# Attention outputs of blocks 1 to 3 in a tile of their own, and block 2's normed tokens transposed ahead through DRAM

## The chip, the core and the metric

The kernel runs on one core of a Trainium2 chip. The metric is the device time of one execution in microseconds (us); the kernel before takes 2342.25 us, the median of 3 runs that lie between 2341.23 and 2342.68.

## What is computed

One layer of a bidirectional encoder. 2,048 tokens and 16 meta tokens in front of them, 1,024 wide, in fp32:

```python
hn   = rms_norm(h, g_mix)
proj = hn @ w_in                      # q: 4 heads, k and v: 2 heads each, u: 4 Fourier groups
attn = block_attention(rope(rms_norm(q)), rope(rms_norm(k)), v)     # every token sees every token
four = fourier_mix(u, w_fourier)      # real part of a 2D DFT over tokens and channels
h    = h + concat(rms_norm(attn, g_attn_out), rms_norm(four, g_fourier_out)) @ w_out
h    = h + relu(rms_norm(h, g_mlp) @ w_up) ** 2 @ w_down            # d_ff = 4096
out  = rms_norm(h, g_final)[meta tokens dropped]
```

## The kernel before, in words

**Arithmetic.** Each fp32 operand of a matmul is split into a high and a low part: ACT makes the high part (a CAST, or an ACTIVATE with a scale, L68 and L71), DVE subtracts it from the source for the low part (L69, L72). A product is then three matmuls, high by high, high by low and low by high (`mm3`, L78 to L80). `split` is such a pair of ACT and DVE instructions. A raw weight tile `wr_...` is loaded through SP's queue and split into `wh_...` and `wl_...` (`wtile`); the rings hold 3 raw tiles (tag `wr`) and 4 of each part (tags `wh` and `wl`), 128x512 each.

**Stages.** Up to about 310 us: projections, norms and rope. Then the Fourier half, beside the first attention units. From there the 2,048 tokens are worked in four blocks of 512 (`BLOCKS`, numbered 0 to 3). Attention is 16 units, two heads of 256 queries each, four units to a block; a unit's result goes to the DRAM tensor `o_d[block]` as high and low parts, one slice of 128x512 for each head `k`. `mix(head(0), ...)` and `mix(head(1), ...)` run the MLP of blocks 0 and 1, and at each `yield` advance attention as far as a schedule says (`n0` and `n1` are the numbers of these yields). When a block's units are done, `out_a(b)` (L917 to L986) runs at the next chance: it loads the block's tokens `h`, multiplies the attention outputs by the attention half of `w_out` in two halves of 512 columns (4 heads by 4 token tiles, PSUM tiles `poa`), adds to `h`, and takes the norm's factor: ACT squares (`hj`), DVE adds up, GpSimd raises to the power -1/2 (`rs_m`, L983). Blocks 2 and 3 then store `h` to `h_d` (L985).

**The operands of `out_a`.** For block 0 they are one tile `at_0` of 16 KB per partition, in the place `e0` of the pool `ey`, which is free then; each slice is loaded once and serves both halves. For blocks 1 to 3, `attn` (L939 to L945) loads each slice into `ath_...` and `atl_...`, tiles of the rings `wh` and `wl`, which they share with the weights, and loads it again for the second half: 8 slices by 2 halves by 3 blocks, 48 loads of 256 KB.

**The transposed tokens.** The MLP needs the normed tokens with the model dimension on the partitions. For blocks 0 and 1, `transposes` (L988) scales them on ACT (`m`, L997), transposes on PE (`pmt`, L1002) and splits the result into `mT` in `e0` (high) and `e1` (low) of `ey`, which thus hold block 1's operands until `up(1, 7)` ends. For blocks 2 and 3 the MLP is one Strassen-Winograd product over both blocks, 7 products for 8: its token operands are the raw transposed tiles `b11`, `b21` (block 2) and `b12`, `b22` (block 3), and the seven forms made of them (`bf1` to `bf7`; `b_form`, a split of 128x1024 pieces); its weight operands are made by `up_weights` (`wuh`, `wul`) from tiles `R0` and `R1`. `flip` (L1162) makes the raw tiles: DVE scales the tokens in place (L1166), PE transposes (L1170), ACT scales out of PSUM (L1171).

**The order at the hand-over.** After both `mix` calls come `down(1, 6)` and `out_a(3)`; then block 2's tokens are loaded again from `h_d` into `h2_0` and `h2_1`, in the places of `R0` and `R1` (L1175 to L1180); then `up(1, 7)` runs with the two flips between its steps, `up_weights` makes its first four weight forms, forms `1` (in `e0`) and `2` (in `e1`) are split, and `down(1, 7)` runs its two halves with form `5` between and form `6` behind. The tokens' activations of `up` are relu, square and a split (L1028, L1029, L68, L69). `b22t`, a sum used for form `6`, has its own tile in the pool `rb`.

**What sets the order.** The program is written once, and a scheduler orders each engine's instructions by cost and priority; within an engine they then run in that order. A tile's buffer is handed on when its last reader is done. Loads run through SP's queue in order, so that one that waits for its buffer holds up those behind it; attention's loads run through GpSimd's queue. The score tiles `s` and the transposes `pmt` share a PSUM ring of two (tag `S` of `app`).

Of the kernel before, what the change touches and what calls it, by code (L numbers as in the profile page):

```python
# [133 lines left out]
def encoder_block(ctx: ExitStack, tc: tile.TileContext, x, meta, w_in, w_f,  # L134
# [63 lines left out]
    h_d = [dram.tile([P, D], F32, name=f"h_d{t}") for t in range(NT)]  # L198

# [709 lines left out]
    hps = hp0, Lines(tc.alloc_tile_pool(name="hp1", bufs=1, reuse_waits="tile"), small)  # L909
    mp = Lines(tc.alloc_tile_pool(name="mp", bufs=1, reuse_waits="tile"), small)  # L910
# [5 lines left out]
    def out_a(b):  # L916
# [16 lines left out]
        if b == 0:  # L933
            A = ey.tile([P, 2, NQ, 512], R32, name="at_0", tag="e0")
            for k in range(NQ):
                for e in range(2):
                    nc.sync.dma_start(f32v(A[:, e, k]), o_d[b][:, e, k])

        def attn(half, k):  # L939
            if b == 0:  # L940
                return A[:, 0, k], A[:, 1, k]
            a = [wp.tile([P, 512], R32, name=f"at{e}_{b}_{half}_{k}", tag="w" + e, bufs=4) for e in "hl"]
            for e in range(2):
                nc.sync.dma_start(f32v(a[e]), o_d[b][:, e, k])
            return a  # L945

        part = []
        for half in range(2):
# [9 lines left out]
            for k in range(NQ):  # L958
                w = wtile(w_out[k * P:(k + 1) * P, c], f"oa_{b}_{half}_{k}", c_ao(k))
                ops[k] = attn(half, k), w  # L960
# [27 lines left out]
    def transposes(b):  # L988
# [5 lines left out]
        for kk in range(KT // 2):  # L994
# [3 lines left out]
            for i in range(2):  # L998
# [4 lines left out]
                split(mhl[0][:, k, :T * P], mhl[1][:, k, :T * P], ps[:, :T * P], c_mlp(k))  # L1003
            yield
# [75 lines left out]
    def head(b):  # L1080
# [14 lines left out]
        def ahead():  # L1095
            if todo and att.n >= need[todo[0]] + 2:
                yield from out_a(todo.pop())
# [9 lines left out]
    n0, n1 = 8 + 4 + 8 * 15 + 8, 8 + 8 * 13 + 8  # L1107
# [67 lines left out]
    h2 = []  # L1175
    for i in range(2):
        h = sp.tile([P, 2, D], F32, name=f"h2_{i}", tag=f"R{i}")
        for t in range(2):
            nc.sync.dma_start(h[:, t], h_d[8 + 2 * i + t])
            h2.append(h[:, t])  # L1180
    b11, b21 = (ra.tile([P, 4, 512], F32, name=f"b{i}1", tag=f"b{i}1") for i in (1, 2))
    b12, b22, b22t = (rb.tile([P, 4, 512], F32, name=f"b{i}2", tag=f"b{i}2") for i in (1, 2, 3))
    BF = {}

# [24 lines left out]

    def in_pool(pool, name):  # L1210
        t = pool.tile([P, 8, 512], R32, name="bf" + name, tag="bf" + name)
        return [t[:, 0:2], t[:, 2:4]], [t[:, 4:6], t[:, 6:8]]

    def flips():
        yield from flip(2, h2, (b11, b21))
        yield from flip(3, H.pop(3), (b12, b22))

    fl = flips()
# [5 lines left out]
    b_form("1", in_ey(0), b11)  # L1224
# [114 lines left out]
    sl.release()  # L1339
    for p in hps[::-1]:  # L1340
# [267 lines left out]
```

## Time and profile before

| | |
|---|---|
| median of 3 runs (lowest, highest) | 2342.25 us (2341.23, 2342.68) |
| the profiled execution, its time | 2340.36 us |
| its span, first to last instruction | 2338.5 us |
| mean granted clock of TensorE | 0.996 |
| PE busy | 2298.0 us, 98% |
| DVE, ACT, GpSimd busy | 74%, 55%, 7% |
| moved by DMA | 312.56 MB, 134 GB/s |

Busy times are of one execution, each engine on its own; a share near 100% says that the engine rarely stood still, not that its matmuls came at the best pace. The rows by windows show how many instructions started in a stretch of time (in brackets, with an x), the clock granted to TensorE in it (PEclk) and the DMA engines' share. The rows of waits give engine, instruction and line, what it waited for, the microseconds in total, how often, and the longest.

### The profile page before, as it was taken

What the parts mean: (1) busy time and instruction counts of PE and PEld (TensorE: products, weight loads), DVE (VectorE), ACT (ScalarE), POOL (GpSimd) and SP (SyncE); (2) the same over time, 40 slices, a digit from 0 to 9 for tenths busy, and PEclk for the clock granted to TensorE, in tenths of its full rate; (3) what the DMA queues carried; (4) which work ended last, traced back from release to release, by engine and by line L of the source; (5) the groups of instructions that cost most, each with busy time, mean ns of one, the idle gap of its engine ahead of it and who ended that gap; (6) DMA issues with size and microseconds to landing.
All of it is one profiled execution on the core that took longest, in us unless ns stands there. A gap on an engine that the chain in (4) does not pass through costs nothing.

```text
span 2338.5 us, 30433 instructions
## 1 busy us (share of the span) xinstructions
PE 2298.0 (98%) x10774; PEld 1875.1 (80%) x10774; DVE 1720.1 (74%) x2771; ACT 1276.6 (55%) x2395; POOL 165.7 (7%) x211
## 2 busy tenths in 40 slices
PE   8999999999999999999999999999999999999998
PEld 7889887677788888788878788888788888788886
DVE  5435678988777887877897877885685656596786
ACT  6443356644565665566776566663655555443333
POOL 2212120110100000100010100000000000100000
PEclk9999999999999999999999999999999999999999
DMA  6333252543533222443242553224535444764442
GB/s 207 104 112 108 73 156 76 170 148 129 169 115 109 78 86 86 142 130 109 64 167 86 169 180 108 64 83 151 185 117 185 153 144 165 303 209 158 130 133 81
DMA packets 181225, 312.56 MB, mean 134 GB/s; under 512 B 15328, under 2 KB 64192, under 8 KB 180944
## 3 DMA queue, kind: packets, MB, share of 16 engines
q1 hardware_dynamic: 162736, 269.97, 35.2%
q0 software_dynamic: 18336, 40.64, 5.9%
q8 instruction: 85, 1.39, 0.2%
q14 instruction: 68, 0.56, 0.1%
HBM read 232.66 MB, written 77.89 MB: 133 GB/s over the span
## 4 chain that ended last, share of the span: by engine, by line
PE 80%; DMA 2%; DVE 2%; ACT 2%; issue 1%; POOL 0%; SPq 0%; POOLq 0%; DVEq 0%; ACTq 0%
PE pdn L78 5%; PE pdn L80 5%; PE pdn L79 5%; PE pup L80 5%; PE pup L79 5%; PE pup L78 5%; PE o L770 3%; PE ux L78 2%; PE ux L80 2%; PE s L78 2%; PE ux L79 2%; PE s L79 2%; PE s L80 2%; PE dx L78 2%; PE dx L79 2%; PE dx L80 2%
## 5 line engine op out<-in xcount | busy, mean ns | idle before, releaser
L78 PE MATMUL pdn<-wh_dn,ah 128*128 128x512 f32 x512 | 201.3, 396 | 2.1 <-ACT r L1028 1.2
L78 PE MATMUL pup<-mT,wh_up 128*128 128x512 f32 x512 | 201.7, 394 | 0.0
L80 PE MATMUL pup<-mT,wl_up 128*128 128x512 f32 x512 | 200.5, 392 | 0.0
L79 PE MATMUL pdn<-wl_dn,ah 128*128 128x512 f32 x512 | 200.5, 392 | 0.0
L79 PE MATMUL pup<-mT,wh_up 128*128 128x512 f32 x512 | 200.4, 391 | 0.0
L80 PE MATMUL pdn<-wh_dn,al 128*128 128x512 f32 x512 | 200.3, 392 | 0.0
L755 ACT ACTIVATE S<-S 128x512 f32<-128x512 f32 (+1 forms) x261 | 162.6, 629 | 59.3 <-DVE S L749 57.8
L749 DVE TENSOR_TENSOR S<-S,mb 128x512 f32<-128x512 f32 (+1 forms) x272 | 180.9, 683 | 16.4 <-ACT mb L742 16.3
L713 ACT COPY S<-s 128x512 f32<-128x512 f32 (+1 forms) x272 | 158.2, 583 | 57.0 <-PE s L80 51.0
L720 DVE TENSOR_TENSOR M<-M,S 128x512 f32<-128x512 f32 (+1 forms) x240 | 165.0, 687 | 26.8 <-ACT S L713 24.0
L68 ACT CAST wh_up<-wr_up 128x512 fp32r<-128x512 f32 x128 | 79.0, 620 | 141.5 <-PE pup L79 75.9
L69 DVE TENSOR_TENSOR wl_up<-wr_up,wh_up 128x512 fp32r<-128x512 f32 x128 | 87.3, 686 | 68.0 <-ACT wh_up L68 60.4
L68 ACT CAST wh_dn<-wr_dn 128x512 fp32r<-128x512 f32 x128 | 79.3, 620 | 101.4 <-PE pdn L80 52.9
L69 DVE TENSOR_TENSOR wl_dn<-wr_dn,wh_dn 128x512 fp32r<-128x512 f32 x128 | 87.6, 686 | 60.8 <-ACT wh_dn L68 52.1
L78 PE MATMUL s<-q,kt 128*128 128x512 f32 (+1 forms) x272 | 128.1, 471 | 3.5 <-ACT S L755 2.1
L68 ACT CAST ah<-a 128x1024 fp32r<-128x1024 f32 x56 | 58.4, 1048 | 112.7 <-issue 60.8
L69 DVE TENSOR_TENSOR pl<-S,ph 128x512 fp32r<-128x512 f32 x165 | 112.5, 686 | 9.7 <-ACT ph L68 7.7
L78 PEld LDWEIGHTS pdn<-wh_dn,ah 128*128 128x128 f32 x512 | 96.7, 189 | 25.3 <-ACT r L1028 4.6
L68 ACT CAST ph<-S 128x512 fp32r<-128x512 f32 x165 | 101.3, 617 | 27.7 <-PE o L80 23.1
L776 DVE TENSOR_TENSOR acc<-acc,S 128x512 f32<-128x512 f32 x165 | 112.8, 683 | 0.4 <-ACT S L755 0.4
L80 PEld LDWEIGHTS pdn<-wh_dn,al 128*128 128x128 f32 x512 | 96.3, 188 | 20.1 <-DVE al L69 0.4
L79 PEld LDWEIGHTS pdn<-wl_dn,ah 128*128 128x128 f32 x512 | 96.5, 188 | 19.5
(322 smaller groups left out, 6339.0 us busy)
## 6 DMA issues: line engine op xcount, KB each, us to landing
wr_up<-in_w_up_dram SPq DMA_DIRECT2D x128, 256.0 KB, 2.8
wr_dn<-in_w_down_dram SPq DMA_DIRECT2D x128, 256.0 KB, 2.6
a<-s_d SPq DMA_DIRECT2D x42, 512.0 KB, 3.7
R<-in_w_up_dram SPq DMA_DIRECT2D x16, 1024.0 KB, 5.3
s_d<-s SPq DMA_DIRECT2D x64, 256.0 KB, 2.0
d<-in_w_down_dram SPq DMA_DIRECT2D x26, 512.0 KB, 5.0
s_d<-c SPq DMA_DIRECT2D x48, 256.0 KB, 2.3
h<-h_d SPq DMA_DIRECT2D x20, 512.0 KB, 5.3
```

Of the source, the lines that this page charges most:

```text
L68: nc.scalar.copy(hi, src)
L69: nc.vector.tensor_tensor(lo, src, f32v(hi), op=ALU.subtract)
L78: nc.tensor.matmul(out, a[0], b[0], start=first, stop=False, skip_group_check=chain)
L79: nc.tensor.matmul(out, a[0], b[1], start=False, stop=False, skip_group_check=chain)
L80: nc.tensor.matmul(out, a[1], b[0], start=False, stop=last, skip_group_check=chain)
L713: nc.scalar.copy(S[:rows], ps[:rows])
L720: nc.vector.tensor_tensor(M[:rows], M[:rows], S[:rows], op=ALU.max)
L749: nc.vector.tensor_tensor(S, S, s["mb"][:rows], op=ALU.subtract)
L755: nc.scalar.activation(p, S, AF.Exp, scale=ISQ)
L770: nc.tensor.matmul(s["O"], v[:, i % 4], p, start=i == 0, stop=False)
L776: nc.vector.tensor_tensor(acc, acc, p, op=ALU.add)
```

## The change

- A pool `atp` with one tile of 16 KB (tag `at`) holds the attention outputs of blocks 1, 2 and 3 in turn, in the form that block 0 had: 8 loads of 256 KB a block, each slice once, both halves of `out_a` read it. `attn` goes, and the rings `wh` and `wl` hold weights alone.
- `flip_early(2)` follows `out_a(2)` inside `head(1)`: for each pair of slices of the model dimension, four ACT scalings of 128x256, eight transposes into the PSUM ring of the scores, two ACT scalings out of PSUM and two stores of 256 KB to the DRAM tensor `m_d`, and a yield (four in all, so `n1` is 124 for 120). `flip(2)` goes: 4 scalings of 128x1024 on DVE, 32 transposes and 8 scalings out of PSUM between the steps of `up(1, 7)`; `flip(3)` stays there. `b11` and `b21` are loaded from `m_d`, 1 MB each; the reload of block 2's tokens (4 loads of 512 KB) goes, so `R0` and `R1` are free for the weights earlier.
- Form `1` is made in the tile `at`, which is free after `out_a(3)`, instead of in `e0`, which is free only after `up(1, 7)`; `b22t` moves into `e0`. The pool `rb` shrinks by 8 KB, and `atp` is released at the end of the seven products.

```diff
@@ -196,6 +196,7 @@
     v_n = dram.tile([P, NKV, NT, P], F32, name="v_n")
     v_m = dram.tile([MR, NKV, P], F32, name="v_m")
     h_d = [dram.tile([P, D], F32, name=f"h_d{t}") for t in range(NT)]
+    m_d = dram.tile([P, KT, 512], F32, name="m_d")
 
 
     def tbank(name, shape=(P, 512)):
@@ -907,6 +908,7 @@
 
 
     hps = hp0, Lines(tc.alloc_tile_pool(name="hp1", bufs=1, reuse_waits="tile"), small)
+    atp = Lines(tc.alloc_tile_pool(name="atp", bufs=1, reuse_waits="tile"), small)
     mp = Lines(tc.alloc_tile_pool(name="mp", bufs=1, reuse_waits="tile"), small)
     H, MT = {}, {}
 
@@ -930,19 +932,10 @@
         nc.vector.tensor_copy(ss[:, :T], ps)
         ra = rstd_of(mp, ss[:, :T], T, 512, "a")
         sums = [mp.tile([P, 2], F32, name=f"hss_{b}_{t}", tag="hss", bufs=8) for t in range(T)]
-        if b == 0:
-            A = ey.tile([P, 2, NQ, 512], R32, name="at_0", tag="e0")
-            for k in range(NQ):
-                for e in range(2):
-                    nc.sync.dma_start(f32v(A[:, e, k]), o_d[b][:, e, k])
-
-        def attn(half, k):
-            if b == 0:
-                return A[:, 0, k], A[:, 1, k]
-            a = [wp.tile([P, 512], R32, name=f"at{e}_{b}_{half}_{k}", tag="w" + e, bufs=4) for e in "hl"]
+        A = (atp if b else ey).tile([P, 2, NQ, 512], R32, name=f"at_{b}", tag="at" if b else "e0")
+        for k in range(NQ):
             for e in range(2):
-                nc.sync.dma_start(f32v(a[e]), o_d[b][:, e, k])
-            return a
+                nc.sync.dma_start(f32v(A[:, e, k]), o_d[b][:, e, k])
 
         part = []
         for half in range(2):
@@ -957,7 +950,7 @@
 
             for k in range(NQ):
                 w = wtile(w_out[k * P:(k + 1) * P, c], f"oa_{b}_{half}_{k}", c_ao(k))
-                ops[k] = attn(half, k), w
+                ops[k] = (A[:, 0, k], A[:, 1, k]), w
                 if k < NQ - 2:
                     for t in range(T):
                         products(t, k)
@@ -1001,6 +994,23 @@
                 for t in range(T):
                     nc.tensor.transpose(ps[:, t * P:(t + 1) * P], m[t // 2][:, t % 2, i * P:(i + 1) * P], ident)
                 split(mhl[0][:, k, :T * P], mhl[1][:, k, :T * P], ps[:, :T * P], c_mlp(k))
+            yield
+
+    def flip_early(b):
+
+        hs, ms = H.pop(b), MT[b]
+        for kk in range(KT // 2):
+            m = [a_tile(f"m_{b}_{i}_{kk}").rearrange("p (t e) -> p t e", t=2) for i in range(2)]
+            for t in range(4):
+                nc.scalar.activation(m[t // 2][:, t % 2], hs[t][:, kk * 256:(kk + 1) * 256], AF.Copy, scale=ms[t])
+            for i in range(2):
+                k = 2 * kk + i
+                ps = app.tile([P, 512], F32, name=f"pmt_{b}_{k}", tag="S", bufs=2)
+                for t in range(4):
+                    nc.tensor.transpose(ps[:, t * P:(t + 1) * P], m[t // 2][:, t % 2, i * P:(i + 1) * P], ident)
+                raw = a_tile(f"mt_{b}_{k}")
+                nc.scalar.activation(raw, ps, AF.Copy, scale=c_mlp(k))
+                nc.sync.dma_start(m_d[:, k], raw)
             yield
 
     def up(b, grp):
@@ -1094,7 +1104,10 @@
 
         def ahead():
             if todo and att.n >= need[todo[0]] + 2:
-                yield from out_a(todo.pop())
+                c = todo.pop()
+                yield from out_a(c)
+                if c == 2:
+                    yield from flip_early(c)
 
         for grp in range(8 if b == 0 else 7):
             yield from up(b, grp)
@@ -1104,7 +1117,7 @@
                 yield from ahead()
         assert not todo
 
-    n0, n1 = 8 + 4 + 8 * 15 + 8, 8 + 8 * 13 + 8
+    n0, n1 = 8 + 4 + 8 * 15 + 8, 8 + 8 * 13 + 8 + 4
     a0, a2 = need[0] + LEAD, need[3] + 1
     a1 = a0 + (a2 - a0) * n0 // (n0 + n1)
     att.cap = need[0] + AHEAD
@@ -1172,15 +1185,12 @@
             if k % 2:
                 yield
 
-    h2 = []
-    for i in range(2):
-        h = sp.tile([P, 2, D], F32, name=f"h2_{i}", tag=f"R{i}")
-        for t in range(2):
-            nc.sync.dma_start(h[:, t], h_d[8 + 2 * i + t])
-            h2.append(h[:, t])
     b11, b21 = (ra.tile([P, 4, 512], F32, name=f"b{i}1", tag=f"b{i}1") for i in (1, 2))
-    b12, b22, b22t = (rb.tile([P, 4, 512], F32, name=f"b{i}2", tag=f"b{i}2") for i in (1, 2, 3))
+    b12, b22 = (rb.tile([P, 4, 512], F32, name=f"b{i}2", tag=f"b{i}2") for i in (1, 2))
+    b22t = ey.tile([P, 4, 512], F32, name="b32", tag="e0")
     BF = {}
+    for b, k in ((b11, 0), (b21, 4)):
+        nc.sync.dma_start(b, m_d[:, k:k + 4])
 
     def b_form(name, tiles, src):
 
@@ -1207,21 +1217,21 @@
         return tuple([wp.tile([P, 1, 512], R32, name=f"bf{e}{name}_{i}", tag="w" + e, bufs=4) for i in range(4)]
                      for e in "hl")
 
+    def in_at(name):
+        t = atp.tile([P, 2, 4, 512], R32, name="bf" + name, tag="at").rearrange("p l k n -> p (l k) n")
+        return [t[:, 0:2], t[:, 2:4]], [t[:, 4:6], t[:, 6:8]]
+
     def in_pool(pool, name):
         t = pool.tile([P, 8, 512], R32, name="bf" + name, tag="bf" + name)
         return [t[:, 0:2], t[:, 2:4]], [t[:, 4:6], t[:, 6:8]]
 
-    def flips():
-        yield from flip(2, h2, (b11, b21))
-        yield from flip(3, H.pop(3), (b12, b22))
-
-    fl = flips()
+    fl = flip(3, H.pop(3), (b12, b22))
     for _ in up(1, 7):
         next(fl, None)
     drain(fl)
     UW = up_weights()
     ready = [next(UW) for _ in range(4)]
-    b_form("1", in_ey(0), b11)
+    b_form("1", in_at("1"), b11)
     b_form("2", in_ey(1), b21)
     drain(down(1, 7, (0,)))
     minus(b11, b12, b11)
@@ -1337,6 +1347,7 @@
     pc.release()
     sl4.release()
     sl.release()
+    atp.release()
     for p in hps[::-1]:
         p.release()
     wp.release()
```

Three places show how instructions move. First SP's queue where block 1's attention outputs are loaded (`o_d` is the DRAM tensor, `wr_oa` the raw weights of `w_out`'s attention half), before and then after:

```order
L793 DMA o_d1_3464<-oh_7_9125 128x2x256
L793 DMA o_d1_3464<-ol_7_9126 128x2x256
L881 DMA wr_oa_1_0_0_9457<-in_w_out_dram 128x512
L881 DMA wr_oa_1_0_1_9496<-in_w_out_dram 128x512
L881 DMA wr_oa_1_0_2_9535<-in_w_out_dram 128x512
L944 DMA ath_1_0_0_9463<-o_d1_3464 128x512
L944 DMA atl_1_0_0_9464<-o_d1_3464 128x512
L881 DMA wr_oa_1_0_3_9545<-in_w_out_dram 128x512
L881 DMA wr_oa_1_1_0_9637<-in_w_out_dram 128x512
L944 DMA atl_1_0_1_9503<-o_d1_3464 128x512
L944 DMA ath_1_0_1_9502<-o_d1_3464 128x512
L944 DMA ath_1_0_2_9541<-o_d1_3464 128x512
```

```order
L882 DMA wr_oa_1_0_0_9453<-in_w_out_dram 128x512
L794 DMA o_d1_3465<-oh_7_9197 128x2x256
L794 DMA o_d1_3465<-ol_7_9198 128x2x256
L938 DMA at_1_9440<-o_d1_3465 128x512 x4
L882 DMA wr_oa_1_0_1_9488<-in_w_out_dram 128x512
L882 DMA wr_oa_1_0_2_9506<-in_w_out_dram 128x512
L882 DMA wr_oa_1_0_3_9512<-in_w_out_dram 128x512
L882 DMA wr_oa_1_1_0_9600<-in_w_out_dram 128x512
L882 DMA wr_oa_1_1_1_9635<-in_w_out_dram 128x512
L882 DMA wr_oa_1_1_2_9670<-in_w_out_dram 128x512
```

The loads of `ath` and `atl`, spread between the weights, are now one load `at_1` of four slices, directly behind the store of the last unit (four more stand further ahead in the queue), and the weights follow in one run.

Second, ACT's order at the hand-over from `up(1, 7)` to `down(1, 7)` (`r` and `ah` are the activations of its four feature tiles, `pup` and `pmt` PSUM tiles, `wuh` weight forms, `b22` block 3's raw tile), before and then after:

```order
L1028 ACTIVATE r_1_7_0_16404<-pup_1_7_0_16152 128x512
L1029 ACTIVATE r_1_7_0_16404<-r_1_7_0_16404 128x512
L68 CAST ah_1_7_0_16407<-r_1_7_0_16404 128x512
L1171 ACTIVATE b22_16150<-pmt_3_4_16368,cols_94 128x512
L1171 ACTIVATE b22_16150<-pmt_3_5_16374,cols_94 128x512
L1028 ACTIVATE r_1_7_1_16411<-pup_1_7_1_16153 128x512
L68 CAST wuh6_0_16448<-us2_0_16445 128x1024
L1029 ACTIVATE r_1_7_1_16411<-r_1_7_1_16411 128x512
L68 CAST wuh5_0_16452<-us1_0_16444 128x1024
L1171 ACTIVATE b22_16150<-pmt_3_6_16392,cols_94 128x512
L1171 ACTIVATE b22_16150<-pmt_3_7_16398,cols_94 128x512
L68 CAST ah_1_7_1_16414<-r_1_7_1_16411 128x512
```

```order
L1038 ACTIVATE r_1_7_0_16371<-pup_1_7_0_16171 128x512
L1039 ACTIVATE r_1_7_0_16371<-r_1_7_0_16371 128x512
L68 CAST ah_1_7_0_16374<-r_1_7_0_16371 128x512
L1038 ACTIVATE r_1_7_1_16378<-pup_1_7_1_16172 128x512
L1039 ACTIVATE r_1_7_1_16378<-r_1_7_1_16378 128x512
L68 CAST ah_1_7_1_16381<-r_1_7_1_16378 128x512
L68 CAST wh_dn_1_7_0_2_16479<-wr_dn_1_7_0_2_16477 128x512
L1038 ACTIVATE r_1_7_2_16385<-pup_1_7_2_16173 128x512
L68 CAST bf1_16428<-b21_16165 128x1024
L1039 ACTIVATE r_1_7_2_16385<-r_1_7_2_16385 128x512
L68 CAST bf1_16428<-b21_16165 128x1024
L68 CAST ah_1_7_2_16388<-r_1_7_2_16385 128x512
```

Before, four scalings out of PSUM and two weight forms of 128x1024 stand between the cast of tile 0 (`ah_1_7_0`) and that of tile 1 (`ah_1_7_1`); now the activations of tiles 0 and 1 stand in one run, and one weight cast and the two pieces of form `2` (`bf1`) are all that stands among those of tile 2. The scalings and the weight forms have moved ahead of these rows.

Third, PE's order at the first transposes of `flip_early(2)` (`o` and `s` are attention's products, `pup_1_2` is `up(1, 2)`); all of it is new here, since before no transposes stood in this stretch:

```order
L78 MATMUL pup_1_2_0_13278<-mT0_1_11385,wh_up_1_2_0_13284 128x512
L79 MATMUL o_12_12632<-pl_12_13_13203,vt_4_1_3_10126 128x512
L80 MATMUL o_12_12632<-ph_12_13_13202,vt_4_1_3_10126 128x512
L79 MATMUL pup_1_2_0_13278<-mT1_1_11386,wh_up_1_2_0_13284 128x512
L1010 MATMUL pmt_2_0_13145<-ident_96,m_2_0_0_13139 128x128
L1010 MATMUL pmt_2_1_13153<-ident_96,m_2_0_0_13139 128x128
L80 MATMUL pup_1_2_0_13278<-mT0_1_11385,wl_up_1_2_0_13285 128x512
L1010 MATMUL pmt_2_0_13145<-ident_96,m_2_0_0_13139 128x128
L1010 MATMUL pmt_2_1_13153<-ident_96,m_2_0_0_13139 128x128
L78 MATMUL pup_1_2_1_13279<-mT0_1_11385,wh_up_1_2_0_13284 128x512
L1010 MATMUL pmt_2_0_13145<-ident_96,m_2_1_0_13140 128x128
L1010 MATMUL pmt_2_1_13153<-ident_96,m_2_1_0_13140 128x128
```

The transposes stand 14 matmuls behind the last product of `out_a(2)`, each pair between two matmuls of `up(1, 2)`. On ACT the four scalings, the pair of scalings out of PSUM and the next four scalings follow one another with one or two of attention's instructions between, and the cast of weight `wh_up_1_2_3` stands behind the last scaling; PE first needs that weight 18 instructions after the last transpose.

## The prediction

> **What bounds the kernel now.** I read the page first.
>
> ```profile
> span 2338.5 us, 30433 instructions
> PE 2298.0 (98%) x10774; PEld 1875.1 (80%) x10774; DVE 1720.1 (74%) x2771; ACT 1276.6 (55%) x2395; POOL 165.7 (7%) x211
> PE 80%; DMA 2%; DVE 2%; ACT 2%; issue 1%; POOL 0%; SPq 0%; POOLq 0%; DVEq 0%; ACTq 0%
> ```
>
> PE sets the time: it is busy for 98% of the span, and 80% of the chain that ended last is on it. The change takes no matmul away and adds none, since the 32 transposes of block 2 only move. So all that it can win is time in which PE stands still or runs at a lower clock, and 2338.5 - 2298.0 = 40.5 us of idle time is the ceiling for the first. The waits of PE show whose it is.
>
> ```profile
> PE pt L253 <- ACT x L237: 8.9, 2, 8.2
> PE poa L78 <- DMA ath<-o_d: 6.7, 10, 1.8
> PE dy L79 <- DVE bl L69: 2.1, 1, 2.1
> PE s L78 <- ACT S L755: 2.1, 1, 2.1
> PE dx L78 <- ACT ah L68: 1.9, 1, 1.9
> PE pdn L78 <- ACT r L1028: 1.2, 1, 1.2
> PE pdn L78 <- ACT ah L68: 0.8, 1, 0.8
> PE uy L78 <- ACT bf L68: 0.6, 1, 0.6
> ```
>
> The first row is the start of the kernel. Two rows belong to the change: `poa` waits ten times for the loads of `ath`, 6.7 us, and `pdn` and `uy`, at the hand-over from `up(1, 7)` to `down(1, 7)`, wait 1.2 + 0.8 + 0.6 = 2.6 us for ACT. `dx` and `dy` lie near 2030 and 2045 us, in the joint down product, which the change does not reach. Next the table of windows, with an undisturbed stretch first, then the three `out_a`, the hand-over, and the two short stretches at a lower clock.
>
> ```profile
> 700.00:728.00 28.00, 28.00 (x125) 23.20 (x124) 24.80 (x41) 15.41 (x27) 1.44 (x2) 1.00 0.38 114
> 960.00:988.00 28.00, 25.17 (x102) 19.67 (x101) 21.37 (x37) 14.22 (x29) 0.76 (x1) 0.94 0.58 177
> 1308.00:1336.00 28.00, 25.30 (x108) 19.77 (x107) 23.20 (x40) 16.41 (x32) 1.45 (x2) 1.00 0.60 186
> 1636.00:1660.00 24.00, 22.68 (x98) 17.32 (x98) 13.40 (x27) 11.82 (x27) 2.95 (x4) 1.00 0.78 261
> 1676.00:1704.00 28.00, 25.40 (x114) 19.89 (x113) 26.64 (x29) 24.56 (x41) 0.00 (x0) 0.94 0.16 57
> 976.00:980.00 4.00, 4.00 (x12) 3.15 (x11) 1.37 (x3) 1.65 (x3) 0.00 (x0) 0.57 0.33 114
> 1692.00:1696.00 4.00, 3.81 (x10) 3.01 (x11) 4.00 (x6) 3.67 (x7) 0.00 (x0) 0.61 0.13 43
> ```
>
> The undisturbed stretch starts a matmul each 28.00 / 125 = 0.224 us. The count shows the loss better than the busy column, because a matmul's modelled duration (389 to 396 ns in other rows of the page) is longer than this pace, so an idle time looks shorter than what is lost. It also catches the two stretches with PEclk 0.57 and 0.61, where PE counts as busy at half pace.
>
> **What the change can win.** By counts, `out_a(1)` lacks 23 matmuls, 5.2 us (960 to 988); `out_a(2)` lacks 17, 3.8 us (1308 to 1336); `out_a(3)` has 98 where 24.00 / 0.224 = 107 would start, 9 x 0.224 = 2.0 us (1636 to 1660). At the hand-over 24 of the 114 records are transposes, which start much closer together:
>
> ```profile
> 1676.00:1704.00 28.00, 3.05 (x24) 2.60 (x23) 0.00 (x0) 3.81 (x6) 0.94 0.16 57
> 1683.20 1.03 PE L1170 MATMUL pmt<-ident,h 128*128 128x128 f32 x8
> 1683.99 0.48 PE L78 MATMUL pdn<-wh_dn,ah 128*128 128x512 f32 x1
> 1685.22 0.39 PE L80 MATMUL pdn<-wh_dn,al 128*128 128x512 f32 x1
> 1686.38 0.50 PE L78 MATMUL pdn<-wh_dn,ah 128*128 128x512 f32 x1 [0.77 <-ACT ah L68]
> 1690.22 0.73 PE L78 MATMUL uy<-bf,wuh 128*128 128x512 f32 x2 [0.61 <-ACT bf L68]
> 1692.18 0.50 PE L78 MATMUL pdn<-wh_dn,ah 128*128 128x512 f32 x1 [1.23 <-ACT r L1028]
> ```
>
> Eight transposes take 1683.99 - 1683.20 = 0.79 us, 0.1 us each. So 90 x 0.224 + 24 x 0.1 = 22.6 of the 28.0 us are used and 5.4 are lost. The sum by counts is 5.2 + 3.8 + 2.0 + 5.4 = 16.4 us. A lower bound comes from the busy columns: 2.83 + 2.70 + 1.32 + 2.60 = 9.4 us idle, and the two slow stretches lack 17.9 - 12 and 17.9 - 10 starts, 1.3 and 1.8 us, the second partly idle: about 12 us. Some records can be missing, which makes the counts too generous; I take 14.5 us as what is there to win, between 12 and 16.4 and nearer to the counts.
>
> *The waits of `out_a`.* These rows say why `ath` comes late: the load itself is short, and its buffer is what is awaited.
>
> ```profile
> ACT wh_oa L71 <- PE poa L79: 9.4, 4, 3.6
> ath<-o_d SPq DMA_DIRECT2D x24, 256.0 KB, 3.1
> atl<-o_d SPq DMA_DIRECT2D x24, 256.0 KB, 3.5
> o_d<-oh SPq DMA_DIRECT2D x16, 256.0 KB, 2.3
> ```
>
> The first row is ACT's wait from 1300 to 1340: the weights' high parts, in the same ring of four as `ath`, stand still until `poa` gives a tile back. Four tiles hold two steps' worth of weight and operand, so a load can only be issued when the product two steps back is done, and lands 3.1 us later, against 12 matmuls, 2.7 us, of a step. With a tile of its own the whole operand is asked for at once, and the rings hold four steps of weights. What stays is the distance from the last unit's store, 2.3 us, and the load, 3.5 us, to the first product: in the new order 88 and 116 PE rows stand between that unit's last transposition and the products with heads 0 and 2 in `out_a(1)`, some 20 us at 0.224 each; `out_a(2)` has 98 rows for its late heads, `out_a(3)` 103. `out_a(0)`, which works in this form already, has no row at all among PE's waits. I leave 0.7 us of the 11 (bounds 0 and 3), mostly for the weights, which now have the ring alone.
>
> *The hand-over.* PE waits there for ACT, which is 24.56 of 28.00 us busy, with DVE at 26.64. From these engines the change takes block 2's share:
>
> ```profile
> L1171 ACT ACTIVATE b<-pmt,cols x16: 672/682/705, 1658.6 to 1685.1; 128x512 f32<-128x512 f32 x16
> L1166 DVE TENSOR_SCALAR h<-h,rs_m 128x1024 f32<-128x1024 f32 x3 | 2.3, 752 | 1.3 <-DMA h_d<-h 1.3
> L68 ACT CAST bf<-b 128x1024 fp32r<-128x1024 f32 x6 | 6.4, 1064 | 0.0
> ```
>
> ACT loses 8 x 0.682 = 5.5 us, DVE 4 x 0.752 = 3.0. Besides, the four weight forms are made before `out_a(3)`, and block 3's scalings end some 24 matmuls ahead of the end of `up(1, 7)`. So after `pup` of tile 0 is done, 18 matmuls or 4.1 us remain on PE; ACT needs about 3 x 0.5 for tile 0, 3 x 0.5 for tile 1, a weight cast, and for tile 2 the same and two casts of 1.06: some 7.1 us from the end of tile 0, and PE asks for tile 2 at 4.1 + 24 x 0.224 = 9.5 us. The cover is 2 us. I leave 0.8 us of the 5.4 (bounds 0 and 4). What is late next is form `6`, behind `down(1, 7)` as before.
>
> The half pace goes with the waits if the waits cause it: both slow stretches follow directly on an idle time of PE of 1 to 2 us. The Trainium skill (TensorE: Matmul & The Clock Gate, in the section Why this matters for your kernels) sees it otherwise: it warns of idle gaps of over about 3 us, and no gap here is that long. By that rule the slow stretches would have another cause and stay, and the sum would be about 3 us less; that is a rival below.
>
> **What the change adds.** *`flip_early(2)`* puts on ACT 16 scalings of 128x256 and 8 out of PSUM, in a stretch with attention. Their like stands behind `out_a(0)`:
>
> ```profile
> L997 ACT ACTIVATE m<-h,rs_m x32: 493/502/518, 637.5 to 1173.3; 128x256 f32<-128x256 f32 x32
> 637.46 2.90 ACT L997 ACTIVATE m<-h,rs_m 128x256 f32<-128x256 f32 x7
> 640.26 1.24 ACT L71 ACTIVATE mT<-pmt,cols 128x512 fp32r<-128x512 f32 x2
> 636.00:648.00 12.00, 12.00 (x57) 7.96 (x56) 6.53 (x12) 11.71 (x28) 2.90 (x4) 1.00 0.46 134
> 636.00:648.00 12.00, 3.78 (x24) 2.81 (x24) 3.46 (x5) 3.63 (x6) 1.00 0.46 134
> ```
>
> Seven scalings take 2.90 us, 0.41 each, and a pair out of PSUM 1.24. A step is then 4 x 0.41 + 1.24 = 2.9 us on ACT, with attention's copy and cast about 4.0; PE has 8 transposes and 12 matmuls in it, 0.8 + 2.7 = 3.5. So ACT is the slower by 0.5 us a step, 2.0 in all, less what PE can take from the order ahead. In the like stretch, with 24 transposes, PE is busy for 12.00 of 12.00 us while ACT is at 11.71: nothing lost by that column. By counts, 33 matmuls and 24 transposes fill 33 x 0.224 + 2.4 = 9.8 us, so up to 2.2 are lost, though slower plain fp32 products of attention are among them. I take 1.0 us (bounds 0 and 4). Two things queue behind it. On ACT the cast of weight `wh_up_1_2_3` stands behind the last scaling, and PE needs it 18 instructions after the last transpose, 4 us, against two scalings, cast and DVE's subtraction, 1.24 + 0.6 + 0.7 = 2.5 us: covered. On SP the eight stores to `m_d` wait for ACT with the loads of weights 6 and 7 behind them, first used 60 PE rows after the last transpose, 13 us, against a store's issue and a load of about 5 us: covered too.
>
> The Trainium skill (TensorE: Matmul & The Clock Gate, Part 4: PE-mode transpose) says that transposes do not count as busy for the clock in the same way, which speaks against strewing them over attention; the row above, granted clock 1.00 over 24 of them, does not show it, and by the rule one slow stretch more would cost under 2 us.
>
> *DMA.* Away go 24 loads of 256 KB and 4 of 512 KB, 8 MB; 2 MB of stores and 2 MB of loads come. The loads of `b11`, `b21` and the first `R` stand in SP's queue ahead of three weights of `down(1, 6)`, where the reload of `h2` stood in like manner, and their buffers come free no later than its did. I cost them at nothing, with 0 to 2 us as bounds.
>
> The sum is -14.5 + 0.7 + 0.8 + 1.0 = -12.0, from 2340.36 us of the profiled execution to 2328.4. The median of the runs lies 1.9 us over that execution, so I forecast **2330 us**, 0.5% less. Its own range is 2326 to 2335.
>
> **The rivals.** *Clock stays* (2333 us): the waits go, but slow stretches come as often, set off by other short gaps, as near 2045 us. It gives back 1.3 + 1.8 = 3.1 us.
>
> *The waits move* (2338 us, or 2341 if all of it does): `out_a` then waits for `wr_oa`, which stands behind the eight loads in one queue, and the hand-over for casts that have only moved. For it: SP's loads come in bursts, with 261 GB/s in 1636 to 1660. Against it: `out_a(0)`. Eight of 14.5 us would return. This takes in the case that the change doesn't reach what it is aimed at.
>
> *Lock-step* (2348 us, slower): in `flip_early` ACT runs in order and the PSUM ring has two places, which scores and transposes share. If at each of the four steps PE stands until ACT has done scalings and PSUM reads, it loses 2.9 us a step, 11.6, and each such gap could bring a slow stretch of up to 1.8 us, 7.2 more: 18.8 in the place of 1.0, so 2330 + 17.8 = 2348. It decides once the four steps lose over 1.0 + 12.0 + 4.7 us in all, where 4.7 us is 0.2% of the median, about what a measurement of this kernel can tell from no change. For it: ACT's 11.71 of 12.00. Against it: PE's 12.00 of 12.00 in the same row.
>
> **How the numbers follow.** My forecast has a chance of 0.60; clock stays 0.15; the waits move 0.18, half of it under 2337.6 us (0.06) or within 0.2% (0.12); lock-step 0.07. So faster is 0.60 + 0.15 + 0.06 = 0.81, the same 0.12, slower 0.07. The range runs from 2324, with the counts' full 16.4 won and nothing added (2340.4 - 16.4 = 2324.0; the median's 1.9 us is left off as slack), to 2340, which takes in most of the moved waits.
>
> **What would show it.** In the new profile the row `poa <- DMA` should be gone or under 1 us, windows over the three `out_a` should hold some 123 starts in 28 us at clock 1.00, and `pdn <- ACT r` and `pdn <- ACT ah` should be gone. In the 16 us after `out_a(2)` PE should be idle for under 1.5 us. I am wrong if `poa` waits for `wh_oa` or `wl_oa` instead, if `pmt` or `s` show waits for ACT of over 4 us, or if stretches at half clock are as many as before while the waits are gone.

## The result, and the profile after

The changed kernel takes 2325.3 us, the median of 6 runs between 2324.01 and 2328.63, against 2341.88 us for the kernel before in 6 runs. The ratio is 0.993, with a 95% interval from 0.9918 to 0.9943: 16.6 us or 0.7% faster, where 12 us were forecast. The profiled execution is the slowest of the six, 2328.63 us.

The page of the changed kernel, its span, busy times and the chain that ended last:

```profile
span 2326.9 us, 30382 instructions
PE 2291.3 (98%) x10774; PEld 1875.5 (81%) x10774; DVE 1716.3 (74%) x2767; ACT 1283.2 (55%) x2411; POOL 168.1 (7%) x211
PE 90%; DVE 3%; DMA 2%; ACT 2%; issue 1%; POOL 1%; SPq 0%; DVEq 0%; POOLq 0%; ACTq 0%
```

PE still runs 10774 matmuls. The chain's share on PE, 90% for 80% before, says nothing of the change: the same kernel has 93% in e1, and e7, with the waits gone too, has 78%. Six rows of the waits of PE in the changed kernel:

```profile
PE pt L254 <- ACT x L238: 8.8, 2, 8.1
PE dy L79 <- DVE bl L69: 3.8, 1, 3.8
PE s L78 <- DMA q<-q_d: 3.4, 2, 2.2
PE dx L78 <- ACT ah L68: 1.9, 1, 1.9
...
PE ux L78 <- ACT p L1321: 0.6, 1, 0.6
...
PE pmt L1183 <- DVE h L1179: 0.4, 1, 0.4
```

The rows of `poa` for `ath` and of `pdn` and `uy` for ACT are gone. New is a short wait of block 3's transposes for their scaling on DVE, 0.4 us; longer are `dy`, 3.8 us where it was 2.1, and `s` for the loads of `q`, which changes from one execution to the next (1.1 us before, 3.4 here, 1.2 in e2). The windows of the changed kernel over `out_a(1)`, `out_a(2)`, `out_a(3)`, the hand-over from `up(1, 7)` to `down(1, 7)`, and the 25 us behind `out_a(2)` with the early transposes:

```profile
957.00:985.00 28.00, 28.00 (x125) 23.18 (x124) 27.47 (x49) 19.41 (x40) 2.49 (x3) 1.00 0.36 111
1300.00:1328.00 28.00, 28.00 (x125) 23.18 (x124) 27.69 (x51) 19.77 (x40) 4.56 (x5) 1.00 0.39 120
1625.00:1647.00 22.00, 22.00 (x102) 18.34 (x101) 12.05 (x24) 8.88 (x19) 2.00 (x2) 1.00 0.36 116
1664.00:1692.00 28.00, 28.00 (x125) 23.12 (x124) 21.48 (x27) 18.88 (x35) 0.00 (x0) 1.00 0.25 76
1329.00:1354.00 25.00, 25.00 (x124) 19.51 (x124) 14.58 (x26) 22.23 (x47) 2.75 (x4) 1.00 0.79 262
```

125 starts in 28 us, at clock 1.00, are just the pace of the undisturbed stretch before: nothing is lost any more in `out_a(1)`, in `out_a(2)` and at the hand-over. The table below has the same for `out_a(3)`, the shorter third row.

To set the stretches of all kernels beside each other, I added up over the matmuls of a stretch how much later than usual the next one started (usual is 0.228 us after a matmul of 512 columns, 0.10 after a transpose). This loss holds idle time and half clock alike. In us:

| stretch | before | after | own operands only (e3) | early flip and forms (e4) | form 1 back (e5) | forms only (e6) | loaded twice (e7) |
|---|---|---|---|---|---|---|---|
| `out_a(1)` | 5.2 | -0.1 | -0.1 | 4.4 | -0.1 | 4.0 | -0.1 |
| `out_a(2)` | 3.7 | -0.1 | -0.1 | 3.1 | -0.1 | 4.0 | -0.1 |
| `out_a(3)` | 3.0 | 0.0 | 0.0 | 3.6 | 0.0 | 2.8 | 0.1 |
| 25 us behind `out_a(2)` | 0.2 | 1.3 | 0.2 | 1.4 | 1.3 | 0.2 | 2.3 |
| `up(1, 7)` | 0.7 | 1.2 | 0.7 | 0.9 | 0.6 | 0.7 | 1.6 |
| hand-over, `down(1, 7)` | 5.3 | -0.1 | 1.3 | -0.1 | 0.2 | 2.5 | -0.1 |
| start of the joint down product | 6.1 | 10.1 | 7.7 | 7.7 | 7.7 | 6.1 | 7.6 |

Of before, `out_a(1)` and the hand-over hold one stretch at half clock each (1.7 us). The column of after says: 12.1 us won in `out_a` and 5.4 at the hand-over, 1.1 + 0.5 paid behind `out_a(2)` and in `up(1, 7)`, 15.9 net, beside 16.6 between the medians. Of the 17.5 us won, 3.4 are the two stretches at half clock of that one execution of before.

### The profile page after: what moved, and what is told of

Same layout as the page of the kernel before. It is cut to its first block, busy times and chain, and to the rows that moved or that the text cites. A ratio compares the mean times of both kernels' runs of the same rounds, so it can differ in the third digit from the quotient of the medians.

```text
span 2326.9 us, 30382 instructions
## 1 busy us (share of the span) xinstructions
PE 2291.3 (98%) x10774; PEld 1875.5 (81%) x10774; DVE 1716.3 (74%) x2767; ACT 1283.2 (55%) x2411; POOL 168.1 (7%) x211
## 4 chain that ended last, share of the span: by engine, by line
PE 90%; DVE 3%; DMA 2%; ACT 2%; issue 1%; POOL 1%; SPq 0%; DVEq 0%; POOLq 0%; ACTq 0%
PE pdn L78 5%; PE pdn L79 5%; PE pdn L80 5%; PE pup L80 5%; PE pup L79 5%; PE pup L78 5%; PE o L771 3%; PE s L78 2%; PE s L79 2%; PE s L80 2%; PE ux L78 2%; PE dx L78 2%; PE ux L79 2%; PE dx L79 2%; PE ux L80 2%; PE dx L80 2%
## 5 line engine op out<-in xcount | busy, mean ns | idle before, releaser
L79 PEld LDWEIGHTS pup<-mT,wh_up 128*128 128x128 f32 x512 | 96.2, 188 | 19.4
```

The source lines that it names most:

```text
L79: nc.tensor.matmul(out, a[0], b[1], start=False, stop=False, skip_group_check=chain)
```

## The experiments

The theory at the start: two separate terms, the ring waits of `out_a` and ACT's load at the hand-over, the second relieved by taking block 2's flip out of it. A first question was the joint down product, where the profile after loses 4 us more than before: a side effect of the change, or chance?

**The changed kernel again (e1)**, with no edit.

> The changed kernel once more, for its spread and a second profile. Its first profile lost 10.1 us of PE time between the last up product and the first 40 us of the joint down product, where the kernel before lost 6.1: dy waited 3.8 us for DVE's low part bl (2.1 before). Theory A, the change does it (the down weights d lie where the tile at was, so they and three loads of a from s_d are issued about 7 us earlier and meet the last stores to s_d): dy waits over 3 us again and the loss is about 10 us again, time 2325. Theory B, it was that one run: dy waits about 2 us, the loss is about 6, span about 4 us shorter than the first profile's 2326.9.

Measured 2326.74 us (2325.4 to 2327.92), before 2341.84, ratio 0.9938 (0.9925 to 0.995). Its waits of PE at that place:

```profile
PE dy L79 <- DVE bl L69: 2.1, 1, 2.1
PE dx L78 <- ACT ah L68: 1.9, 1, 1.9
```

`dy` waits 2.1 us as before, and the loss there is 6.0 us. The 3.8 us were that one execution: theory B.

**Late loads of the down weights (e2).** With the tile `at` in the pool stack, `d11` to `t2` lie on forms 1 and 3 rather than 3 and 4, and their loads are issued earlier. An unused tile ahead of them puts them back: a batch of four loads goes out 10.4 us behind the first ones then, as before the change (10.5), instead of 3.5 in e1.

```diff
             if g == 0:
                 own2("a")
+                dn.tile([P, 3584], F32, name="pad", tag="pad")
                 load(1, 1)
```

> The changed kernel with an unused tile of 14 KB ahead of d11, so that d11 to t2 lie on the last two forms again, as in the kernel before, and are loaded as late as there. Nothing else moves. Theory A (early loads meet the stores): dy waits about 2 us, the loss at the start of the joint down product falls from 10 to about 6 us, time about 2321 to 2322. Theory B (chance): the time is that of the changed kernel, 2325 within 1 us, and the loss varies from profile to profile.

Measured 2326.44 us (2323.56 to 2328.12), ratio 0.9935 (0.9923 to 0.9947), loss there 6.1 us, `dy` 2.1. The same as e1 without the edit: the earlier loads cost nothing that shows, theory B again.

**Own operands, block 2's flip as before (e3).** The reload of block 2's tokens comes back with it; forms 1 and `b22t` stay where the change puts them.

```diff
-                c = todo.pop()
-                yield from out_a(c)
-                if c == 2:
-                    yield from flip_early(c)
+                yield from out_a(todo.pop())
...
-    fl = flip(3, H.pop(3), (b12, b22))
+    def flips():
+        yield from flip(2, h2, (b11, b21))
+        yield from flip(3, H.pop(3), (b12, b22))
```

> Attention outputs in a tile of their own, form 1 in it and b22t in e0, but block 2's flip as before: reloaded from h_d, transposed during up(1, 7). Theory A (out_a's waits and the hand-over are two separate terms, and block 2's flip makes the second): the three out_a lose under 1 us (12.1 before), the hand-over still 4 to 5.5 us, time 2342 - 12 = 2330, 2328 to 2332. Rival (the hand-over is paid by the place of form 1 and b22t, not by the flip): the hand-over loses under 1.5 us and the time is 2324 to 2326.

Measured 2326.34 us (2323.97 to 2330.64), ratio 0.9938 (0.9926 to 0.9951): the time of the whole change, not 2330. The window of e3 at the hand-over:

```profile
1674.40:1702.40 28.00, 27.63 (x123) 21.89 (x122) 27.87 (x34) 20.06 (x37) 0.00 (x0) 1.00 0.15 47
```

With DVE at 27.87 of 28.00 us PE still idles only 0.37 and the loss is 1.3 instead of 5.3. So my theory was wrong on the second term: the hand-over gets better with block 2's flip still in it, as the rival has it. In the table, the early flip wins another 1.4 us there and pays 1.1 behind `out_a(2)` and 0.5 in `up(1, 7)`: nothing in sum. The times (2326.74 and 2326.34 on one chip) agree, as far as intervals of some 3 us to either side can say.

**Early flip and forms, operands through the rings (e4).** `attn` stands as before the change.

```diff
-        A = (atp if b else ey).tile([P, 2, NQ, 512], R32, name=f"at_{b}", tag="at" if b else "e0")
+        if b == 0:
+            A = ey.tile([P, 2, NQ, 512], R32, name="at_0", tag="e0")
...
+            a = [wp.tile([P, 512], R32, name=f"at{e}_{b}_{half}_{k}", tag="w" + e, bufs=4) for e in "hl"]
...
-                ops[k] = (A[:, 0, k], A[:, 1, k]), w
+                ops[k] = attn(half, k), w
```

> Block 2 flipped early through DRAM, form 1 in the tile at, but out_a's operands loaded through the weight rings, twice, as before. Theory A: the three out_a lose their 12 us again, the hand-over under 1 us, the early flip costs 1 us: 2342 - 5.4 + 1.0 = 2337.5, 2335.5 to 2339.5. Rival (the early flip needs the free rings, or loses more beside the waits of out_a(2)): over 3 us lost in the 25 us after out_a(2), time 2340 or more.

Measured 2338.14 us in 11 runs (2335.9 to 2339.75), ratio 0.9986 (0.9977 to 0.9995). Its waits of PE for the operands:

```profile
PE poa L78 <- DMA ath<-o_d: 6.3, 8, 2.2
PE poa L80 <- DMA atl<-o_d: 1.3, 2, 0.8
```

The waits are back, 11.1 us of loss without any stretch at half clock among them, and the hand-over loses nothing. Theory A, to within a microsecond.

**Form 1 back in `e0` (e5)**, with the early flip kept.

```diff
-    b22t = ey.tile([P, 4, 512], F32, name="b32", tag="e0")
+    b22t = atp.tile([P, 4, 512], F32, name="b32", tag="at")
...
-    b_form("1", in_at("1"), b11)
+    b_form("1", in_ey(0), b11)
```

> The changed kernel with form 1 made in e0 again, behind up(1, 7), and b22t in the tile at; the early flip stays. So far the hand-over lost 5.3 us before, 1.3 with own tile and forms but block 2's flip inside, and nothing with all. Theory A (ACT's load there has a threshold; either relief brings it nearly under): with the flip out but form 1's two casts and two subtractions back in, the hand-over loses 0 to 1.5 us, time 2325 to 2328. Rival (form 1's place is what pays): the hand-over loses 3 us or more and the time is 2329 or more.

Measured 2325.41 us (2322.3 to 2326.98), ratio 0.9928 (0.9914 to 0.9941). The window at the hand-over:

```profile
1674.00:1702.00 28.00, 27.95 (x124) 22.79 (x123) 27.20 (x32) 17.47 (x31) 0.00 (x0) 1.00 0.14 48
```

0.2 us of loss, as theory A has it. So with `out_a`'s operands out of the rings either relief is enough nearly by itself: the flip moved out (e5), or form 1 made elsewhere (e3, 1.3 us). Neither run shows them without the free rings; e6 does for form 1.

**The forms alone (e6).** e3 and e4 together: operands through the rings, flip inside, only form 1 and `b22t` moved; the edit against the kernel before.

```diff
-    b12, b22, b22t = (rb.tile([P, 4, 512], F32, name=f"b{i}2", tag=f"b{i}2") for i in (1, 2, 3))
+    b12, b22 = (rb.tile([P, 4, 512], F32, name=f"b{i}2", tag=f"b{i}2") for i in (1, 2))
+    b22t = ey.tile([P, 4, 512], F32, name="b32", tag="e0")
...
-    b_form("1", in_ey(0), b11)
+    b_form("1", in_at("1"), b11)
```

> Of the change only the tile at, used for form 1 alone, with b22t in e0: out_a's operands go through the weight rings twice, block 2's flip is inside up(1, 7). Theory A: out_a's three waits stay at 12 us, the hand-over loses 1.3 us as it did with own operands (5.3 before): 2342 - 4 = 2338, within 1.5. Rival (the better hand-over came from the rings or the queue left free, not from form 1's place): the hand-over loses 4 us or more, time 2341 to 2343.

Measured 2339.54 us in 11 runs (2335.63 to 2345.47), ratio 0.9992 (0.9984 to 1.0001): by its time hardly told from no change. The window at the hand-over and the longest wait in it:

```profile
1681.80:1709.80 28.00, 26.75 (x118) 20.77 (x118) 27.87 (x33) 20.92 (x38) 0.00 (x0) 1.00 0.16 49
```

```profile
PE pdn L78 <- ACT r L1029: 0.9, 1, 0.9
```

The loss is 2.5 us, between the two expectations (1.3 and 4), with no half clock. Before loses 3.6 us here without its slow stretch, so form 1's place alone wins 1.1; with the rings free too, in e3, 1.3 us are left, 1.2 less than here. ACT's order around the activations is the same in e3 and e6, but counted from the last product of `up(1, 7)`, each cast of `ah` there ends 1.1 us later in e6. Ahead of them ACT waits for the load of a weight form's source, longer in e6 (the first row) than in e3:

```profile
ACT wuh L68 <- DMA R<-in_w_up_dram: 2.1, 1, 2.1
```

```profile
ACT wuh L68 <- DMA R<-in_w_up_dram: 0.8, 1, 0.8
```

These 1.3 us are about the 1.2 that the loss differs by. That this wait is the cause is likely, not shown; nor is what makes the load land later.

**Loaded twice into the own tile (e7).**

```diff
                 w = wtile(w_out[k * P:(k + 1) * P, c], f"oa_{b}_{half}_{k}", c_ao(k))
+                if b and half:
+                    for e in range(2):
+                        nc.sync.dma_start(f32v(A[:, e, k]), o_d[b][:, e, k])
```

> The changed kernel, but out_a's second half loads each slice again into its own place of the tile at: the same 48 loads of 256 KB as before, without the weight rings. Theory A (the rings made the wait, not the repeated traffic): no wait of poa over 0.3 us, the three out_a lose under 1 us together, time that of the changed kernel, 2325 to 2327. Rival (loading once is what pays): poa waits for the second loads, 3 us or more in all, time 2329 or more.

Measured 2327.25 us (2324.66 to 2330.7), ratio 0.9939 (0.9927 to 0.9952). Its loads, and its windows over `out_a(1)` and `out_a(2)`:

```profile
at<-o_d SPq DMA_DIRECT2D x56, 256.0 KB, 4.3
```

```profile
956.00:984.00 28.00, 28.00 (x125) 23.20 (x124) 27.48 (x49) 19.27 (x40) 2.41 (x3) 1.00 0.58 186
1301.00:1329.00 28.00, 28.00 (x125) 23.19 (x124) 26.77 (x50) 19.08 (x40) 4.04 (x4) 1.00 0.60 195
```

56 loads (48 and block 0's 8) where the changed kernel has 32, the DMA share at 0.58 and 0.60 as before the change, and not one start missing. What paid in `out_a` is the buffer that isn't shared with the weights, not that it is loaded once. Behind `out_a(2)` and in `up(1, 7)` e7 loses 1.4 us more than the changed kernel; whether the second loads do that, one profile can't say. Whether rings with more places, still shared, would do as well as a buffer apart, no run shows.

**The early flip's scalings on DVE (e8).**

```diff
-                nc.scalar.activation(m[t // 2][:, t % 2], hs[t][:, kk * 256:(kk + 1) * 256], AF.Copy, scale=ms[t])
+                nc.vector.tensor_scalar(m[t // 2][:, t % 2], hs[t][:, kk * 256:(kk + 1) * 256], ms[t], None, op0=ALU.mult)
```

> The changed kernel with the 16 scalings of the early flip on DVE instead of ACT. The 25 us after out_a(2) lose 1.25 us in the changed kernel and 0.2 without the early flip. Theory A (ACT paces these steps): the loss falls to 0.5 or less. Rival (ACT is not what PE waits for; the loss is many pieces of 0.1 us where transposes stand singly between matmuls): the loss stays at 0.8 to 1.3 or follows how the transposes are grouped. The time does not tell them apart: 2325 to 2327 in both.

Measured 2325.79 us (2323.98 to 2326.59), ratio 0.9931 (0.9919 to 0.9944), loss behind `out_a(2)` 1.3 as with ACT. The window:

```profile
1329.00:1354.00 25.00, 25.00 (x123) 19.71 (x123) 21.10 (x46) 17.93 (x35) 4.65 (x5) 1.00 0.78 273
```

ACT goes from 22.23 to 17.93 us and PE's loss stays. Theory A falls: ACT is not what costs that microsecond. No single loss in that stretch is over 0.3 us. In the changed kernel it is 17 groups of one to four transposes between matmuls, 0.01 to 0.09 us each and 0.6 together, and four matmuls without a transpose directly ahead, 0.10 to 0.15 us later than usual each and 0.5 together. What delays these four is open.

**GpSimd at the start of the joint down product (e9, e10)**, with the changed kernel once more beside them (e11). This is not part of the change; it goes for the largest stall that all versions have behind the start of the kernel. In e10 only the first edit stands, in e9 both.

```diff
-                        split(hi, lo, r)
+                        if g == 0 and name == "2" and x == "a":
+                            nc.scalar.copy(hi, r)
+                            nc.gpsimd.tensor_tensor(lo, r, f32v(hi), op=ALU.subtract)
+                        else:
+                            split(hi, lo, r)
...
-            sub(t1, raw[1, 2], raw[1, 1])
-            sub(t2, raw[2, 2], t1)
+            for h in range(2):
+                eng = nc.gpsimd if g == 0 else nc.vector
+                eng.tensor_tensor(t1[h], raw[1, 2][h], t1[h], op=ALU.subtract)
+                eng.tensor_tensor(t2[h], raw[2, 2][h], t1[h], op=ALU.subtract)
```

> An attempt at the largest stall that the change leaves: at the start of the joint down product PE loses 6 to 10 us in every profile, two gaps of 2.3 (dy waits for DVE's bl) and 2.0 us (dx waits for ACT's ah, which stands behind sums on DVE) with up to two stretches at half clock of 1.7 us each. The changed kernel, with the low parts of a2 and the sums t1 and t2 of the first group on GpSimd, which stands idle there. Theory A (DVE's order makes both gaps): both shrink, the loss there falls by 3 us or more, time 2320 to 2323. Rival (GpSimd is slow, and its queue holds the loads of d12, d22 and a behind the low parts): the second gap grows, time 2326 or more.

> As the run before, with only the low parts of a2 on GpSimd; the sums stay on DVE. Theory A: the first gap (dy for bl, 2.3 us) goes, the second stays at 2.0 or comes earlier, time 2322 to 2325. Rival: a load held behind the low parts on GpSimd makes the second gap longer, time 2326 or more.

> The changed kernel once more beside these two, for their comparison and a third profile: 2325 to 2327, 15 to 16 us under the kernel before. In the joint down product the same two gaps of 2.3 and 2.0 us, each with or without a stretch at half clock behind it, by where it falls on the grid of 3.41 us on which these stretches lie.

e9: 2330.53 us (2327.85 to 2332.05), ratio 0.9952 (0.9938 to 0.9966), loss 9.1 us. e10: 2322.88 (2321.95 to 2324.59), ratio 0.9918 (0.9905 to 0.9932), loss 3.9. e11: 2325.29 (2324.2 to 2327.02), ratio 0.9929 (0.9916 to 0.9941), loss 7.7. The waits in this stretch in e9, and GpSimd's work in it:

```profile
PE dx L79 <- DVE bl L69: 4.6, 1, 4.6
PE dy L79 <- DVE bl L69: 2.0, 2, 1.0
```

```profile
2005.11 4.77 POOL L1402 TENSOR_TENSOR al<-a,ah 128x1024 fp32r<-128x1024 f32 x2 [13.81 <-ACT ah L1401]
2009.83 2.89 POOL L1369 DMA_DIRECT2D d<-in_w_down_dram  x4
2012.71 1.10 POOL L1377 DMA_DIRECT2D a<-s_d  x2
2014.28 5.94 POOL L1434 TENSOR_TENSOR d<-d,d 128x1024 f32<-128x1024 f32 x2 [0.47 <-DMA d<-in_w_down_dram]
2020.18 4.77 POOL L1435 TENSOR_TENSOR t<-d,d 128x1024 f32<-128x1024 f32 x2
```

And the waits there in e10:

```profile
PE dx L78 <- ACT ah L68: 1.7, 1, 1.7
PE dy L79 <- DVE bl L69: 1.0, 1, 1.0
```

GpSimd takes 2.4 to 3.0 us for a subtraction that takes DVE 1.22. The low parts alone take two of them off DVE's line, and the first gap shrinks from 2.1 to 1.0 us. In e9 the four sums make the second gap 4.6, so the rival's time holds there. Of its two reasons only GpSimd's pace is borne out: the loads behind the low parts start as late in e10 as in e9, and its second gap is 1.7 us; in e9 GpSimd waits 0.5 us for them. The last four loads of `d` in e10, then the last six in the changed kernel:

```profile
2008.13 2.89 POOL L1369 DMA_DIRECT2D d<-in_w_down_dram  x4
```

```profile
1989.38 2.86 POOL L1369 DMA_DIRECT2D d<-in_w_down_dram  x4 [2.02 <-PE ux L79]
1996.66 1.43 POOL L1369 DMA_DIRECT2D d<-in_w_down_dram  x2 [4.42 <-ACT c L1260]
```

e10 is 2.4 us under the changed kernel beside it (e11). Their intervals against before overlap, so this step is probable rather than shown; against the kernel before, e10 is the fastest of all. Of the 3.8 us between the losses of e10 and e11 here, about 3.3 are two stretches at half clock that e11 has and e10 has not, and the gaps themselves shrink by 1.3 (e10 loses some of it again elsewhere).

## Why the prediction was right, point by point

The forecast was faster by 12 us, 2330 us, and 2325.3 was measured: inside the whole range (2324 to 2340), just under the forecast's own (2326 to 2335), and over a third more gain than forecast. Both terms were there and the order of size is right; the cause of the second was wrong.

- *`out_a`: right.* Waits of `poa` were to vanish with a tile of their own; they did, and e4 and e6 bring them back with the rings. That the ring and not the load is what is awaited was argued from ACT's wait for `poa`; e7 shows it. I left 0.7 us, and nothing is left: the step mis-sized is that remainder, and the counts' 2.0 us for `out_a(3)`, which by start-to-start distances is 3.0.
- *The hand-over: right in sum, wrong in its cause.* 5.4 us were there, I left 0.8 and none was left. But the text had ACT and DVE relieved by block 2's flip; that form 1 leaves ACT's line stands in its sum (two casts where before has four) and not among its reasons. e3 keeps that flip inside and loses 1.3; e5 takes it out, puts form 1 back, and loses 0.2. DVE is not what PE waits for: it is busier in e3 (27.87 us) than before (26.64), and all three waits before are for ACT. Before, the cast of tile 1's `ah` ends 5.7 us after that of tile 0, in e3 and e6 3.3 us, because two casts for weight forms that stood between them come behind them; tile 2's ends 10.1 us after tile 0's, there 8.9. With the rings free either relief is nearly enough, and the second then has little left to win: the two do not add up. The flip moved out alone, rings shared and form 1 in its old place, was not run.
- *The early flip: right in size by luck, wrong in what makes it.* 1.0 us was forecast from ACT's pace of four steps, and 1.1 is lost, but with the scalings on DVE (e8) it is lost as well. Not foreseen were 0.5 us in `up(1, 7)`, where block 3's scalings now come first and PE waits for DVE (the row `pmt <- DVE h`); e5, which flips early too, has neither that row nor the loss, so it hangs on where form 1 and `b22t` lie as well. In sum the early flip has gained nothing here: its 1.4 at the hand-over stands against 1.6.
- *What is there to win: mis-sized.* I took 14.5 us between 12 and 16.4; 17.5 were won. The counts of starts were nearer than the caution about missing records. With the two remainders, 0.7 + 0.8, and 0.6 more paid than forecast, this is the difference between 12.0 and 15.9. Of its side forecasts, the 2341 us for all of the waits moving does not follow from its terms: 2330 and the 13.0 us of waits that it takes as won make 2343. And `dy` lies near 2030 us and `dx` near 2045, not the other way round.
- *Half clock.* The two slow stretches went with their gaps, as forecast, and the rival by which they stay found nothing: in no profile of the changed kernel is there one at either place. But there is none in e4 and e6 either, where the waits of `out_a` are back, so the 3.4 us that they make of the gain in these profiles are partly chance (the last section says on what it hangs). Others, at 585 us and in the joint down product, stay with gaps that the change does not touch.
- *The other rivals.* The waits did not move to `wr_oa`: e7 doubles the loads in front of the weights and loses nothing in the three `out_a` (0.1 us in `out_a(3)`). Lock-step has no trace: in the 25 us behind `out_a(2)` PE is busy for 25.00.

## What to carry to other kernels

Where a stage borrows a ring that another stream runs on, look at who gives the buffer back, not at the load's duration; a place of its own for 16 KB took away all three waits here, and did so even when everything was loaded into it twice. Where two reliefs aim at the same overloaded place, test each alone: once one brings it under the cover, the other has nothing left to win and its own price remains. Compare losses by stretch across profiles, since single executions differ by several microseconds at places that the change does not touch.

## What the runs showed of the hardware

The stretches at half clock last 3.41 us or a multiple, but for the last one, which runs to the end of the kernel, and their starts lie on a grid of 3.41 us: in the profile of before at 586.9, 976.1, 1692.9 and 2044.4 us, which are 0, 114, 324 and 427 steps of 3.4133 from the first. The other twelve profiles have such a grid too, each at a place of its own. A short gap sets one off or not by where it falls on this grid. The same two gaps, of `dy` and `dx`, in the kernel before and then in e1:

```profile
2031.04 0.50 PE L79 MATMUL dy<-bl,ah 128*128 128x512 f32 x1 [2.15 <-DVE bl L69]
2043.18 0.50 PE L78 MATMUL dx<-bh,ah 128*128 128x512 f32 x1 [1.88 <-ACT ah L68]
```

```profile
2016.37 0.80 PE L79 MATMUL dy<-bl,ah 128*128 128x512 f32 x1 [2.15 <-DVE bl L69]
2030.02 0.50 PE L78 MATMUL dx<-bh,ah 128*128 128x512 f32 x1 [1.88 <-ACT ah L68]
```

The windows behind these gaps, in before and in e1 (PEclk is the third number from the right):

```profile
2031.10:2034.50 3.40, 3.40 (x15) 2.83 (x16) 1.20 (x2) 0.00 (x0) 0.00 (x0) 1.00 1.02 410
2044.40:2047.80 3.40, 3.40 (x9) 2.66 (x9) 3.39 (x4) 3.40 (x4) 1.14 (x3) 0.51 0.27 60
```

```profile
2016.20:2019.60 3.40, 3.23 (x8) 2.58 (x9) 1.25 (x2) 0.00 (x0) 0.00 (x0) 0.50 0.55 180
2029.80:2033.20 3.40, 3.18 (x14) 2.47 (x14) 3.38 (x4) 3.40 (x5) 0.53 (x1) 1.00 0.00 0
```

In before the gap of 1.88 us halves the clock and that of 2.15 does not; in e1 it is the other way round. In all profiles of this case, outside the place near 585 us where several gaps follow one another, a single gap of 1.9 to 2.3 us at full clock halved the clock if the last matmul ahead of it started between 0.6 us ahead of a step of the grid and 1.1 us into it, so that the gap lies in one step nearly whole, and did not from 1.1 us on, where it runs over the step's end. The two longer ones, 3.8 us (`dy` after) and 4.6 (`dx` in e9), both halved it, though the second began 1.2 us into a step. A gap of 1.8 us that lies so did it once (`out_a(1)` before) and once not (`out_a(1)` in e6), one of 1.7 did not (`dx` in e10): the edge is about there. The Trainium skill (TensorE: Matmul & The Clock Gate, Part 1: The HAM clock gate) describes a window of 3413 ns that runs free of the kernel, and with this the grid agrees; that only gaps of over about 3 us matter (its section Why this matters for your kernels) these rows contradict: 1.9 us were enough. The grid would also account for part of the spread of one kernel's runs over several us: each such stretch costs 1.7 us, and where the grid lies changes from run to run. The runs fit this without showing it. Each has its mean granted clock on record, which one stretch lowers by 0.0007 (half of 3.41 us in 2338); of 39 runs of before in the experiments, the two at 0.994 take 2346.4 us in the mean, the 13 at 0.995 2342.7, the 20 at 0.996 2341.4 and the four at 0.997 2339.2.
